# Layer 1's latents: the values' PSUM buffers, the engines that empty them, and the rotary key's copy

## The chip, the cores and the metric

The kernel runs on one core of a Trainium2 chip. A core has five engines that each work through their own queue in order: TensorE (PE: matmuls and transposes), VectorE (DVE), ScalarE (ACT), GpSimd (POOL) and SyncE (SP, which here only issues DMAs). Matmuls write to PSUM, which has eight banks of 128 partitions by 512 float32; VectorE and ScalarE carry results from there to SBUF. The metric is the device time of one execution in microseconds, as a median of several.

## The reference, cut to what matters

Two layers over a sequence of 1024 tokens with 1024 features. Layer 0 is differential attention, layer 1 is multi-head latent attention; each is followed by a gated MLP with a causal convolution. The change is in the input side of layer 1's attention:

```python
def mla_attention(h, w_in, q_norm_g, kv_norm_g, w_uq, w_ukv, w_o, cos, sin):
    proj = h @ w_in                                            # 384 + 256 + 32 columns
    c_q = rms_norm(proj[..., :MLA_Q_RANK], q_norm_g)           # the queries' latents
    c_kv = rms_norm(proj[..., MLA_Q_RANK:MLA_Q_RANK + MLA_KV_RANK], kv_norm_g)
    k_pe = apply_rope(proj[..., MLA_Q_RANK + MLA_KV_RANK:], cos, sin)   # the rotary key
    q = (c_q @ w_uq).reshape(b, s, MLA_HEADS, MLA_NOPE + MLA_ROPE)
    kv = (c_kv @ w_ukv).reshape(b, s, MLA_HEADS, MLA_NOPE + MLA_V)
    v = kv[..., MLA_NOPE:]                                     # the values
```

## The kernel before

Every product of float32 matrices is made from three matmuls (`mm3`, lines 116 to 121): both operands are split into a high part and the rest (`hi`, line 127, mostly on ACT; `lo`, line 130, on DVE or POOL), and the product of the two rests is left out. Layer 1's input (`mla_input`, line 1111) runs over eight tiles of 128 tokens. For tile i it does:

- `latents(i)`: 48 matmuls from the normed tokens into the two banks of one tile `S`: the queries' 384 columns in the first bank, the 256 key and value columns and the rotary key's 32 in the second. Then, for each of the two norms, a sum of squares on ACT (L157), its root on DVE (L162) and POOL (L163), and a scaled copy on DVE (L1151) into the SBUF tile `nat`. Last, ACT copies the 32 rotary columns (L1152).
- `turn(i)`: PE transposes `nat` (L1160, L1168, and L1169 for the rotary columns) into tiles `b`, which ACT and DVE split; ACT copies the rotary key (L1173).
- `values(i)`: 12 matmuls into a second tile `S`, one copy by ACT of all 1024 columns (L1184), and a DMA to DRAM (L1185).

Between these stand the transposes of the next tokens (L182). After the eighth tile come the key and query units of the first two heads, the rotary key's rotation (`rotary`: DVE L233, POOL L235 and L236, then ACT's L127 and DVE's L125 copies of 32 rows to the four key tiles, for each half of the tokens), and then attention, in 64 steps of scores (into `S`), softmax (L1449, L1450), POOL's scaling (L149), transposes of the weights (L248, into `b`), their split, and the product with the values (L1470 and L1471, into `u`).

The eight banks are shared by all of this through three tags:

```python
def big(self):
    return self.t(self.ps, "S", [P, 1024], 2)
def bank(self, tag="b"):
    return self.t(self.ps, tag, [P, 512], 1 if tag == "u" else 3)
```

So there are two tiles `S` of two banks, three of one bank under `b`, and one bank under `u`, which `mla_input` does not use before the change. Who follows whom in an engine's queue is not written out here: a scheduler orders the instructions of this part and of attention when the program is built, by its own estimate of when operands and buffers come free. An engine that waits at run time holds up all that is queued behind.

Of the kernel before, what the change touches and what calls it, by code (L numbers as in the profile page):

```python
# [18 lines left out]
P = 128  # L19
S = 1024  # L20
D = 1024
# [35 lines left out]
class Trunk:  # L57
# [1053 lines left out]
    def mla_input(self, W, hts, turns, v_d, heads_of):  # L1111


        nc, a = self.nc, self.a
# [24 lines left out]
        late = SimpleNamespace()  # L1139

        def latents(i):
            acc = self.big()
            for k in range(KD):
                for b, m, kind in ((0, 384, "q"), (512, 288, "kv")):
                    wh, wl = where[kind, k]
                    self.mm3(acc[:, b : b + m], hts[i][:, 0, k, :], hts[i][:, 1, k, :], wh, wl, k == 0, k == KD - 1)
            nat = nats([P, 672])
            for b, m, off, gain in ((0, 384, 0, g[0]), (512, 256, 384, g[1])):
                d = nat[:, off : off + m]
                r = self.rstd(acc[:, b : b + m], d, m)  # L1150
                nc.vector.scalar_tensor_tensor(d, acc[:, b : b + m], r, gain, ALU.mult, ALU.mult)  # L1151
            nc.scalar.copy(nat[:, 640:672], acc[:, 768:800])  # L1152
            return nat

        def turn(i, nat):
# [19 lines left out]
        def values(i):  # L1175
            half = i // 4
            s = slice((i % 4) * P, (i % 4 + 1) * P)
            y = self.big()
            for b in (0, 512):
                for k in range(2):  # L1180
                    ch, cl = (cT.kv(part, half, k)[:, s] for part in range(2))
                    self.mm3(y[:, b : b + 512], ch, cl, late.wv[k][0][:, b : b + 512], late.wv[k][1][:, b : b + 512], k == 0, k == 1)
            vs = self.raw([P, D])
            nc.scalar.copy(vs, y)  # L1184
            nc.sync.dma_start(v_d[:, :, i].rearrange("h p e -> p h e"), vs.rearrange("p (h e) -> p h e", e=P))  # L1185

        def rotary(half):
# [9 lines left out]
        nat = {}  # L1197
        for i in range(NT + 2):
            if i < NT:
                nat[i] = latents(i)  # L1200
                if turns:
                    turns.pop(0)()
            if i in (1, 5):
                latent_tiles(i // 4)
            if i == 3:
                heads = heads_of(cT, kT)
            if i == 2:
                late.tab = self.at("s13", [MLA_ROPE, 2, S])
                nc.sync.dma_start(late.tab, a["rope_k"])
            if i == 1:  # L1210

                late.wv = [self.split(f"s{4 + k}", self.fetch(a["mla_wuv"][k * P : (k + 1) * P, :], D)) for k in range(2)]
            if i == 6:
                kT += [self.at(place, [P, 2, S], F32R) for place in ("s0", "s1", "s10", "s11")]
            if 0 <= i - 1 < NT:
                turn(i - 1, nat.pop(i - 1))
            if i == NT:
                heads.first(0)
            if i >= 2:
                values(i - 2)  # L1220
            if i in (7, NT + 1):
                rotary(i // NT)
# [517 lines left out]
```

## Time and profile before

| what | us |
|---|---|
| median of 3 runs (lowest to highest) | 2480.05 (2479.67 to 2480.57) |
| span of the profiled execution | 2476.8 |
| PE busy in it | 2376.1 (96%) |
| DVE, ACT, POOL busy | 1899.8, 1301.3, 651.6 |
| mean granted PE clock | 0.992 of full speed |
| the latents' stage of layer 1 | about 1258 to 1347 |
| its tail: values, first heads' units, rotary key | 1347 to 1376 |
| attention of layer 1 | about 1376 to 1700 |

The profiled execution's own time is not listed apart from its span; the median stands 3.25 us above the span, for what lies before the first and after the last instruction. All times within the program count from the span's start. A row of the time line is: start, length, engine, line, operation, the tile written and the tiles read, and in brackets how long the engine was idle before it and what ended that. A row of the waits is: the waiting engine, tile and line, what it waited for, the total, how often, and the longest.

### The profile page before, as it was taken

The numbers are of one execution on the slowest core, as the hardware profiler recorded it, in microseconds if no ns is written. First come the engines' busy times: TensorE is split into PE (matmuls) and PEld (weight loads), VectorE is DVE, ScalarE is ACT, GpSimd is POOL, SyncE is SP. The second block draws the span as 40 slices with busy tenths as digits, with TensorE's granted clock in tenths as the row PEclk, the third lists the DMA queues.
The fourth block names the chain that finished last, engine by engine and source line by source line (L and its number), as shares of the span: only waits on it lengthen the run. The fifth ranks groups of instructions, "written<-read, shape, count | busy, mean of one in ns | idle before, by whom it ended". The sixth has DMA issues, their size and how long they took to land.

```text
span 2476.8 us, 32625 instructions
## 1 busy us (share of the span) xinstructions
PE 2376.1 (96%) x11960; PEld 2007.7 (81%) x11960; DVE 1899.8 (77%) x3078; ACT 1301.3 (53%) x2417; POOL 651.6 (26%) x512
## 2 busy tenths in 40 slices
PE   6999999899999999999999999999999999999998
PEld 5788787788888888788888788888888888887886
DVE  6667776846788888899853787777368888888997
ACT  5677777844444444444434777776244444444443
POOL 5545554526000000000131666656350000000001
PEclk9999999899999999999999999999999999999999
DMA  4111111314222222543221211113222222227401
GB/s 154 43 35 43 35 35 44 128 59 132 64 83 83 80 90 80 216 159 104 81 90 52 75 39 35 42 54 119 93 85 94 77 85 84 87 77 280 166 5 77
DMA packets 95104, 214.44 MB, mean 87 GB/s; under 512 B 8640, under 2 KB 33856, under 8 KB 94784
## 3 DMA queue, kind: packets, MB, share of 16 engines
q1 hardware_dynamic: 86048, 185.09, 22.4%
q10 hardware_dynamic: 8896, 27.27, 3.0%
q8 instruction: 94, 1.54, 0.3%
q14 instruction: 66, 0.54, 0.1%
HBM read 159.89 MB, written 52.43 MB: 86 GB/s over the span
## 4 chain that ended last, share of the span: by engine, by line
PE 77%; DVE 8%; ACT 6%; issue 3%; DMA 3%; POOL 2%; SPq 0%; ACTq 0%; POOLq 0%; DVEq 0%
PE S L119 13%; PE S L120 13%; PE S L121 13%; PE b L119 8%; PE b L120 8%; PE b L121 8%; PE u L119 3%; PE u L120 3%; PE u L121 3%; PE b L248 2%; ACT u L1381 1%; PE b L182 1%; PE u L1471 1%; PE u L1470 1%; DVE s L130 1%
## 5 line engine op out<-in xcount | busy, mean ns | idle before, releaser
L163 POOL TENSOR_TENSOR st<-st,mhalf 128x1 f32<-128x1 f32 x56 | 33.8, 605 | 1314.0 <-DVE st L162 1304.9
L127 ACT CAST u<-h 128x512 fp32r<-128x512 f32 (+2 forms) x242 | 146.1, 619 | 279.6 <-DVE h L630 255.7
L119 PE MATMUL S<-s,u 128*128 128x512 f32 (+1 forms) x752 | 285.8, 380 | 5.7 <-DVE u L768 3.9
L121 PE MATMUL S<-s,u 128*128 128x512 f32 (+1 forms) x752 | 284.1, 378 | 0.0
L120 PE MATMUL S<-s,u 128*128 128x512 f32 (+1 forms) x752 | 284.0, 378 | 0.0
L119 PE MATMUL b<-s,u 128*128 128x512 f32 x588 | 231.6, 394 | 0.5
L120 PE MATMUL b<-s,u 128*128 128x512 f32 x588 | 229.5, 390 | 0.0
L121 PE MATMUL b<-s,u 128*128 128x512 f32 x588 | 229.4, 390 | 0.0
L678 DVE SCALAR_TENSOR_TENSOR u<-u,conv,u 128x1023 f32<-128x1023 f32 (+1 forms) x176 | 225.2, 1279 | 1.6 <-ACT u L674 1.6
L149 POOL TENSOR_TENSOR u<-u,st 128x384 f32<-128x384 f32 (+7 forms) x160 | 170.1, 1070 | 152.2 <-DVE st L1456 100.8
L119 PE MATMUL u<-s,s 128*128 128x512 f32 x432 | 174.7, 404 | 14.7 <-ACT h L416 6.7
L130 DVE TENSOR_TENSOR u<-b,u 128x512 fp32r<-128x512 f32 (+1 forms) x256 | 158.7, 632 | 38.2 <-ACT u L127 35.7
L127 ACT CAST s<-u 128x512 fp32r<-128x512 f32 (+3 forms) x196 | 128.6, 693 | 96.5 <-PE u L121 35.4
L121 PE MATMUL u<-s,s 128*128 128x512 f32 x432 | 170.2, 394 | 0.0
L120 PE MATMUL u<-s,s 128*128 128x512 f32 x432 | 169.6, 393 | 0.0
L119 PEld LDWEIGHTS S<-s,u 128*128 128x128 f32 x752 | 141.4, 188 | 34.2 <-issue 4.4
L121 PEld LDWEIGHTS S<-s,u 128*128 128x128 f32 x752 | 141.4, 188 | 26.3
L120 PEld LDWEIGHTS S<-s,u 128*128 128x128 f32 x752 | 141.4, 188 | 25.9
L127 ACT CAST u<-b 128x512 fp32r<-128x512 f32 (+1 forms) x256 | 133.8, 550 | 50.1 <-PE b L248 46.3
L681 ACT ACTIVATE u<-u 128x1024 f32<-128x1024 f32 x44 | 46.7, 1062 | 197.2 <-DVE u L678 197.2
L248 PE MATMUL b<-ident,u 128*128 128x128 f32 x864 | 138.3, 277 | 7.9 <-DVE u L130 5.7
L130 DVE TENSOR_TENSOR u<-h,u 128x512 fp32r<-128x512 f32 x162 | 111.4, 688 | 33.0 <-ACT u L127 31.8
(254 smaller groups left out, 6646.5 us busy)
## 6 DMA issues: line engine op xcount, KB each, us to landing
u<-in_ffn_up SPq DMA_DIRECT2D x88, 512.0 KB, 3.8
g_d<-u ACTq DMA_DIRECT2D x44, 512.0 KB, 2.6
u<-in_ffn_down SPq DMA_DIRECT2D x66, 256.0 KB, 5.3
u<-g_d SPq DMA_DIRECT2D x62, 256.0 KB, 4.4
s<-in_da_wqkv SPq DMA_DIRECT2D x24, 512.0 KB, 3.6
x_d<-u SPq DMA_DIRECT2D x16, 512.0 KB, 2.9
s<-x_d SPq DMA_DIRECT2D x8, 1024.0 KB, 8.9
u<-o_d SPq DMA_DIRECT2D x24, 256.0 KB, 2.8
```

Of the source, the lines that this page charges most:

```text
L119: mm(out, lh, rl, start=first, stop=False, skip_group_check=onto)
L120: mm(out, lh, rh, start=False, stop=False, skip_group_check=onto)
L121: mm(out, ll, rh, start=False, stop=last, skip_group_check=onto)
L127: self.nc.scalar.copy(out, src)
L130: (eng or self.nc.vector).tensor_sub(out, src, hi.bitcast(F32))
L149: self.nc.gpsimd.tensor_mul(x, x, s.to_broadcast(list(x.shape)))
L163: nc.gpsimd.tensor_tensor(r, s, self.mhalf, ALU.pow)
L182: self.nc.tensor.transpose(ps[:, k * P : (k + 1) * P], src[:, k * P : (k + 1) * P], self.ident)
L248: self.nc.tensor.transpose(ps[:, j * P : (j + 1) * P], probs[t][:, k : k + P], self.ident)
L678: nc.vector.scalar_tensor_tensor(t[half][:, back:], u[half][:, : S - back], w, t[half][:, back:], ALU.mult, ALU.add)
L681: nc.scalar.activation(t[0], t[0], AF.Silu)
L1381: nc.scalar.activation(e, sc[c], AF.Exp, bias=nm[:, c : c + 1], accum_out=l[:, c : c + 1])
```

## The change

In `values`, the two halves of 512 columns get a single bank each, the first under `u` and the second under `b`, and each half is copied out alone, the first by VectorE and the second by ScalarE. In `latents`, the copy of the rotary key's 32 columns moves ahead of the norms and from ScalarE to VectorE.

```diff
             nat = nats([P, 672])
+            nc.vector.tensor_copy(nat[:, 640:672], acc[:, 768:800])
             for b, m, off, gain in ((0, 384, 0, g[0]), (512, 256, 384, g[1])):
                 d = nat[:, off : off + m]
                 r = self.rstd(acc[:, b : b + m], d, m)
                 nc.vector.scalar_tensor_tensor(d, acc[:, b : b + m], r, gain, ALU.mult, ALU.mult)
-            nc.scalar.copy(nat[:, 640:672], acc[:, 768:800])
             return nat
...
-            y = self.big()
-            for b in (0, 512):
+            vs = self.raw([P, D])
+            for b, tag, evict in ((0, "u", nc.vector.tensor_copy), (512, "b", nc.scalar.copy)):
+                y = self.bank(tag)
                 for k in range(2):
                     ch, cl = (cT.kv(part, half, k)[:, s] for part in range(2))
-                    self.mm3(y[:, b : b + 512], ch, cl, late.wv[k][0][:, b : b + 512], late.wv[k][1][:, b : b + 512], k == 0, k == 1)
-            vs = self.raw([P, D])
-            nc.scalar.copy(vs, y)
+                    self.mm3(y, ch, cl, late.wv[k][0][:, b : b + 512], late.wv[k][1][:, b : b + 512], k == 0, k == 1)
+                evict(vs[:, b : b + 512], y)
```

In the changed program the lines after the first insertion stand one lower up to the end of the norms, so that L1151 becomes L1152 and the rotary copy is L1148; both value copies have line 1184. The numbers behind a tile's name tell its buffers apart.

The first place is PE's queue at the fourth and fifth group of latents, before the change. S_11182 is the fourth group's tile, S_11291 the second tile of values, S_11307 the fifth group's.

```order
L121 MATMUL S_11182<-u_1872_10783,s_1904_11008 128x288
L182 MATMUL b_11246<-ident,s_1681_9117 128x128 x4
L182 MATMUL b_11253<-ident,s_1681_9117 128x128 x4
L1160 MATMUL b_11276<-ident,u_1921_11111 128x128 x3
L119 MATMUL S_11291<-s_1915_11039,s_1911_11034 128x512
...
L121 MATMUL S_11291<-s_1917_11044,s_1911_11034 128x512
L1168 MATMUL b_11284<-ident,u_1921_11111 128x128 x2
L1169 MATMUL b_11284<-ident,u_1921_11111 32x128
L119 MATMUL S_11307<-u_1864_10739,s_1926_11125 128x384
```

The same place after the change, where S_11184 is the fourth group's tile, S_11311 the fifth's, b_11175 the second half of the first values and u_11294 the first half of the second:

```order
L121 MATMUL S_11184<-u_1872_10783,s_1904_11008 128x288
L119 MATMUL S_11311<-u_1864_10739,s_1926_11125 128x384
...
L120 MATMUL S_11311<-u_1870_10779,s_1926_11125 128x384
L119 MATMUL b_11175<-s_1915_11039,s_1911_11034 128x512
...
L119 MATMUL S_11311<-u_1866_10743,s_1926_11125 128x288
L182 MATMUL b_11248<-ident,s_1681_9117 128x128 x4
L119 MATMUL u_11294<-s_1915_11039,s_1911_11034 128x512
```

The fifth group follows the fourth with nothing between, and the values' matmuls, which stood between two groups, are now strewn into a later group.

The second place is ACT's queue behind the last group of latents, before the change. S_11714, S_11803 and S_11819 are the last three tiles of values; the rows with 32x2x512 are the rotary key's copies.

```order
L1184 COPY u_2009_11727<-S_11714 128x1024
L127 COPY s_1992_11601<-u_2012_11736 32x2x512 x2
L127 COPY s_1994_11603<-u_2012_11736 32x2x512 x2
L127 CAST s_1978_11503<-b_11747 128x2x128
L1152 COPY u_2001_11685<-S_11636 128x32
L1184 COPY u_2023_11816<-S_11803 128x1024
...
L1184 COPY u_2025_11832<-S_11819 128x1024
L127 CAST u_2028_11841<-h_2026_11835 32x512
L127 CAST s_2016_11773<-h_2018_11784 128x512
L127 COPY s_1992_11601<-u_2028_11841 32x2x512 x2
L127 COPY s_1994_11603<-u_2028_11841 32x2x512 x2
```

The same after the change; b_11733, b_11824 and b_11842 are the second halves of the last three values:

```order
L1184 COPY u_2013_11724<-b_11733 128x512
L127 COPY s_1996_11609<-u_2018_11748 32x2x512 x2
L127 COPY s_1998_11611<-u_2018_11748 32x2x512 x2
L127 CAST s_1981_11509<-b_11759 128x2x128
...
L1184 COPY u_2028_11815<-b_11824 128x512
L127 COPY s_1996_11609<-u_2036_11857 32x2x512 x2
L127 COPY s_1998_11611<-u_2036_11857 32x2x512 x2
L1184 COPY u_2031_11833<-b_11842 128x512
```

The last values' copy stood ahead of the second set of rotary copies and now stands behind it.

The third place is PE's queue in attention, before the change, in a head in the middle; b_12925 to b_12949 are transposed weights of one step, u_12888 a product with the values.

```order
L248 MATMUL b_12941<-ident,u_2259_12855 128x128
L119 MATMUL S_13000<-s_1992_11601,s_2206_12624 128x384
...
L248 MATMUL b_12925<-ident,u_2265_12877 128x128
...
L248 MATMUL b_12941<-ident,u_2265_12877 128x128
L1470 MATMUL u_12888<-u_2262_12870,s_2091_12125 128x256
L1471 MATMUL u_12888<-u_2262_12870,s_2091_12125 128x256
...
L248 MATMUL b_12949<-ident,u_2259_12855 128x128
```

The same step after the change, where b_12941 to b_12965 are the four tiles of transposed weights:

```order
L248 MATMUL b_12941<-ident,u_2267_12871 128x128
...
L119 MATMUL S_13016<-s_1996_11609,s_2214_12640 128x384
...
L248 MATMUL b_12949<-ident,u_2267_12871 128x128
...
L119 MATMUL S_13057<-s_1996_11609,s_2214_12640 128x512
...
L248 MATMUL b_12957<-ident,u_2267_12871 128x128
...
L1470 MATMUL u_12904<-u_2270_12886,s_2099_12141 128x256
...
L248 MATMUL b_12965<-ident,u_2267_12871 128x128
```

Before, three tiles were filled in one run of ten transposes and the fourth, which reuses the first one's bank, came after four short matmuls; now the scores of the next steps stand between one tile and the next. No line of attention is edited: the scheduler's order differs here in every head.

## The prediction

> **What bounds the kernel now.** I read the page first, for the engine that sets the time.
>
> ```profile
> PE 2376.1 (96%) x11960; PEld 2007.7 (81%) x11960; DVE 1899.8 (77%) x3078; ACT 1301.3 (53%) x2417; POOL 651.6 (26%) x512
> PEclk9999999899999999999999999999999999999999
> PE 77%; DVE 8%; ACT 6%; issue 3%; DMA 3%; POOL 2%; SPq 0%; ACTq 0%; POOLq 0%; DVEq 0%
> ```
>
> PE is busy for 96% of the span and holds 77% of the chain that ended last, at nearly full clock. So a change pays only where it takes away a wait of PE, and what DVE or ACT save elsewhere is worth nothing. Next I asked for PE's waits over three stretches: the latents' groups (1284 to 1347), the tail and the start of attention (1347 to 1386), and attention's steady part (1440 to 1654).
>
> ```profile
> PE S L119 <- ACT u L1184: 3.3, 3, 1.4
> PE b L1168 <- DVE u L1151: 1.0, 1, 1.0
> ...
> PE S L119 <- ACT u L1450: 4.1, 4, 1.8
> PE S L119 <- ACT s L127: 1.4, 1, 1.4
> PE S L119 <- ACT u L1184: 0.8, 1, 0.8
> ...
> PE b L248 <- DVE u L130: 4.8, 9, 0.9
> ```
>
> In the latents PE loses 3.3 + 1.0 = 4.3 us, nearly all of it to the copy of the values, L1184. In the tail it loses 4.1 + 1.4 + 0.8 = 6.3 us, mostly to the softmax of attention's first steps. In attention nine waits for the split of the transposed weights make 4.8 us. The time line shows how one of the first kind comes about.
>
> ```profile
> 1299.54 1.06 ACT L157 ACTIVATE h<-s 128x1024 bf16<-128x1024 f32 x1
> 1300.59 1.00 ACT L1184 COPY u<-S 128x1024 f32<-128x1024 f32 x1
> 1301.64 0.44 PE L119 MATMUL S<-u,s 128*128 128x384 f32 x1 [1.37 <-ACT u L1184]
> ```
>
> ACT first squares a token tile (1.06 us) and only then copies the values (1.00 us). PE starts the fifth group of latents 0.05 us after that copy, having idled 1.37 us, though the fourth group's tile was long summed. The reason is the count of buffers: two tiles S serve latents and values alike, so each group waits until the values in between are out.
>
> **The change part by part.** The prices come from the groups of ACT and DVE by shape, between 1255 and 1376.
>
> ```profile
> L1184 ACT COPY u<-S 128x1024 f32<-128x1024 f32 x8 | 8.1, 1011 | 2.9 <-issue 2.1 <-PE S L121 0.8
> L127 ACT CAST s<-b 128x512 fp32r<-128x512 f32 x12 | 6.6, 587 | 0.1
> L1152 ACT COPY u<-S 128x32 f32<-128x32 f32 x8 | 1.6, 203 | 1.2 <-DVE u L1151 1.2
> L127 ACT CAST s<-u 32x1024 fp32r<-32x1024 f32 x8 | 8.4, 1047 | 0.8 <-POOL u L130 0.7
> ...
> L1268 DVE TENSOR_TENSOR h<-b,u 128x512 f32<-128x512 f32 x4 | 2.7, 683 | 2.5 <-PE b L121 2.5
> L130 DVE TENSOR_TENSOR h<-b,h 128x128 fp32r<-128x128 f32 x8 | 2.3, 288 | 1.5 <-ACT h L127 1.5
> L125 DVE CAST s<-u 32x1024 fp32r<-32x1024 f32 x8 | 5.5, 685 | 0.1
> L1448 DVE MEMSET S<- 64x64 f32 x3 | 0.3, 112 | 0.0
> ```
>
> *The copies of the values.* ACT's eight copies of 1.011 us go. For each, ACT does one half; the nearest row, a one-bank read of the same size, has 0.587. DVE does the other half, for which before has no plain copy: the nearest is its one-bank multiply with 0.683, and nothing that it runs on this size is cheaper than ACT's 0.587, so I take 0.68 with 0.5 to 0.8 as ends. ACT saves 8 x (1.01 - 0.59) = 3.4 us and DVE gets 5.4 us more. In the latents a bank of values is filled again only a whole group later, 8 us by PE's rows, so neither figure enters the sum there.
>
> *The waits for S.* The values leave S, and latents alternate between its two tiles. A group then needs the tile of the group before the last, which has been read out while 48 matmuls of the last one ran (about 7.4 us at 0.13 to 0.18 each), against some 4 us of squares, roots and scaled copies. In PE's order before, 0.3 to 1.1 us of matmuls stand between the last values and the next group; after, nothing has to be emptied there. The three waits go, **-3.3 us**. What is late next: PE's transposes of the normed tokens, but these stand 2 us or more ahead of their use in the new order. The 1.0 us for L1168 behind L1151 goes too, **-1.0 us**, since that transpose now stands a whole group behind the norm.
>
> *The rotary columns.* ACT's eight copies of 0.203 us go; DVE makes them at once, at a price between its 0.112 (a fill of 64x64) and 0.288 (128x128); I take 0.2. They add a wait: in the new program the first square of each group (L157) waits for this copy, for both write the tile `nat`. Behind that square in ACT's queue stand the splits of the transposes. So each group's norm ends about 0.2 us later, hidden by the 7 us of matmuls in all groups but the last, where it counts below.
>
> *The tail.* I walk the new order from the end of the last group with durations of before, where that end is 1347.3. A matmul of 512 columns counts 0.23 from start to start, as in the two rows of 1348, a transpose 0.105 (ten of them take 1.01 to 1.06 to the next row in the view on attention below).
>
> ```profile
> 1347.57 0.49 ACT L157 ACTIVATE u<-S 128x384 f32<-128x384 f32 x1 [7.17 <-PE b L1169]
> 1348.10 0.40 PE L119 MATMUL S<-s,s 128*128 128x512 f32 x1
> 1348.33 0.39 PE L120 MATMUL S<-s,s 128*128 128x512 f32 x1
> 1348.42 0.55 POOL L163 TENSOR_TENSOR st<-st,mhalf 128x1 f32<-128x1 f32 x1 [9.47 <-DVE st L162]
> 1350.39 1.38 POOL L163 TENSOR_TENSOR st<-st,mhalf 128x1 f32<-128x1 f32 x1
> 1353.16 0.48 DVE L1151 SCALAR_TENSOR_TENSOR u<-S,st,h 128x256 f32<-128x256 f32 x1
> ...
> 1361.21 1.01 ACT L1184 COPY u<-S 128x1024 f32<-128x1024 f32 x1 [2.13 <-issue]
> 1365.51 0.34 SPq L135 DMA_DIRECT2D u<-v_d  x1
> 1376.37 0.79 PE L119 MATMUL S<-s,s 128*128 128x512 f32 x1 [0.25 <-ACT u L1450]
> ```
>
> Before, the chain is: square at +0.3, root, scaled copy, and the same for the second norm; DVE's four rotary copies (4 x 0.685) get in between and stretch POOL's root from 0.55 to 1.38, so the second scaled copy runs at +5.9. After, it runs at about +6.7, because the rotary copy (0.2) and the half of the values (0.68) stand ahead of it on DVE. PE reaches its transpose (L1168) already at 6 x 0.105 + 12 x 0.23 + 3 x 0.105 + 6 x 0.23 = +5.1, since only half of the next values stands between; that is **a new wait of about 2 us**, counted in what follows. ACT's half copy of values ends at +4.1 and its four rotary copies (4 x 1.047) at +8.3; behind the splits of the last transposes, the last values' first half starts at about +9.5 against +10.5, and the rotary rotation that hangs on L1173 starts near +10.4 against +12.2. ACT does not sit behind two more full copies, so the first score of 896 columns, which before starts at 1376.37 = +29.1, comes at about +28, and 0.7 us of transposes that stood behind it are done by then, while 0.5 us of transposes that stood ahead of the last group have moved into the tail. That is 1.1 + 0.7 + 0.5: **-2.3 us**. One thing runs the other way: the last values' copy by ACT now stands behind the second rotary copies and ends near +22 (before, 1362.2 = +14.9). Behind it are the store, the fetch of the values back (SP, 1365.51) and ACT's split of them, which now comes at about +28.5 and has exps queued behind it. That is why I bound the tail at 2 us lost and 4.5 us won.
>
> *Attention.* No line is edited, but the scheduler orders it anew. A step's four tiles of transposed weights share three banks:
>
> ```profile
> 1477.89 1.25 PE L248 MATMUL b<-ident,u 128*128 128x128 f32 x10
> 1478.58 1.07 ACT L127 CAST u<-b 128x512 fp32r<-128x512 f32 x2 [1.22 <-PE b L248]
> 1478.90 0.36 PE L1470 MATMUL u<-u,s 128*128 128x256 f32 x1
> 1479.20 0.56 DVE L1449 TENSOR_REDUCE st<-S 128x1 f32<-128x384 f32 x1
> 1479.68 1.28 DVE L130 TENSOR_TENSOR u<-b,u 128x512 fp32r<-128x512 f32 x2
> 1480.41 0.55 PE L248 MATMUL b<-ident,u 128*128 128x128 f32 x3 [0.86 <-DVE u L130]
> ```
>
> Ten transposes run in one go, four products follow, and the fourth tile waits 0.86 us for the first one's bank: ACT's split, then a maximum (0.56) and two subtractions on DVE. Summing PE's rows from the end of the first tile to the fourth (a matmul by its columns, 0.06 to 0.23) gives 1.0 us before, against a turnround of 1.2 to 1.9 (1.0 plus waits of 0.18 and 0.86 in turn). In the new order the scores between the tiles make it 2.4 us, and the smallest such distance on any bank is 2.0 us; a distance of 1.7 us elsewhere in the old order shows no wait. But DVE's new order puts a maximum ahead of the first subtraction, so the turnround grows to about 2.1. Of the 4.8 us I take 3.4 as gone: **-3.4 us**, with 0 and 5 as ends.
>
> **Sum.** -3.3 - 1.0 - 2.3 - 3.4 = -10.0 us, from a span of 2476.8 to 2466.8. The median of the runs lies 3.25 us above that span, so **2470.0 us**, 0.40% less. About 0.2% (5 us) is what a measurement of this kernel can tell from no change.
>
> **The clock.** The granted clock is a cost that the order of the waits decides.
>
> ```profile
> core 0: us, PE busy (x) PEld busy (x) DVE busy (x) ACT busy (x) POOL busy (x), PEclk, DMA share, GB/s
> 1357.06:1360.48 3.42, 2.64 (x10) 1.91 (x11) 2.86 (x7) 1.68 (x5) 0.22 (x1) 1.00 0.56 158
> 1370.72:1374.13 3.41, 1.62 (x9) 1.03 (x7) 3.36 (x5) 3.39 (x6) 2.45 (x2) 1.00 0.00 0
> 1374.13:1377.55 3.42, 2.31 (x8) 1.71 (x7) 3.34 (x9) 2.11 (x7) 3.42 (x2) 0.50 0.41 153
> 1377.55:1380.96 3.41, 3.41 (x12) 2.83 (x11) 1.79 (x4) 1.95 (x4) 3.41 (x4) 0.50 0.52 154
> ```
>
> A stretch of 3.41 us in which PE was busy 1.62 is followed by two at half clock, while one with 2.64 is not. Half clock over the 5.7 us of busy time behind it costs 2 to 3 us. The sum leaves it as it is, for the new walk has two waits of over 1 us between +25 and +28, as before. The Trainium skill, "TensorE: Matmul & The Clock Gate", Part 1, says that the array falls back to half rate after an idle window of about 3.4 us that runs freely, and advises against gaps above that. The length of the stretches agrees; the gap does not, since here 1.79 us of waiting was enough. By the page no wait of the new tail would cost any clock, and the sum would be 2467.5; by the rows it stays 2470.0.
>
> **The rivals.**
>
> *A second fall of the clock, and no gain in attention.* The new wait of 2 us for L1168 falls within one such stretch and halves the clock: 3 us of the time back. With attention's waits staying too, -6.6 + 3 = -3.6 us, 2476.4. For it: 1.79 us of waiting did it at 1374. Against: the 2 us must lie in one stretch, and the distances in attention's order are plain.
>
> *No fall at all.* The tail's new waits (2, 0.5, 1.2 and 1.3 us) are spread over five or more stretches, and none holds 1.8 us of them: 2.5 us of the old loss go as well, 2467.5. For it: the 1.36 us of waiting in the stretch at 1357 cost nothing. Against: the last two waits are within 3.4 us of each other. The page above speaks for it, the row at 1370 against.
>
> *The tail takes it all.* The values come back 7 us later, exps queue behind their split, and the gain of the latents only lengthens waits that end at a fixed time: 4.3 + 2.3 us are lost, attention keeps its 3.4 or not: 2476.7 to 2480. For it: ACT's queue is strict. Against: the chain through POOL's rotation, which set the start before, gets shorter.
>
> *Slower.* The new order of attention puts a wait into every head. The place is the fourth tile of weights, where DVE's maximum stands ahead of the subtraction that frees the bank. If two maxima and a late split come together, the turnround is 1.9 + 0.56 + 0.64 = 3.1 us against a distance of 2.0: 1.1 us in each of 14 heads, 15.4 us in place of the 4.8. The sum is then -6.6 - 4.8 + 15.4 = +4.0, 2484.1, and with a second such place in a head over 2490. It decides from (6.6 + 4.8) / 14 = 0.8 us a head. Against: the longest turnround seen is 1.9.
>
> *The change does nothing.* The scheduler could have kept values and latents in turn. Its order shows otherwise, and it would give 2480.
>
> **How the numbers follow.** The forecast has 0.48 (2465 to 2474), no fall 0.12, the second fall 0.18, the tail 0.13, slower 0.06, nothing 0.03. The range for 8 in 10 takes in the ends of tail and attention on the side of the forecast and most of the second fall: 2464 to 2478. Faster by over 0.2% (below 2475.1): the forecast, no fall, and half of the second fall, 0.70 in all with a little of the tail. Same: 0.25. Slower: 0.05.
>
> **What would show it.** In the changed trace, no wait for L1184 ahead of a group of latents, and the last group's end near 1342.5 (0.5 us of transposes moved behind it). One wait for L1168 of some 2 us behind it. Attention's first score of 896 columns near 1370.5. In attention, waits for L130 under 1.5 us in all. The prediction is wrong if PE waits for DVE's copy under `u`, if the clock falls twice, or if a wait comes back in every head.

## The result, and the profile after

| | before | after |
|---|---|---|
| median, us (lowest to highest) | 2480.31 (2479.67 to 2484.03) | 2462.72 (2462.70 to 2463.07) |
| ratio, 95% interval | | 0.9929 (0.9915 to 0.9943) |
| span of the profiled execution, us | 2476.8 | 2460.9 |

The change takes 17.6 us off, 0.71%. The forecast was 2470.0 us, 10 us less than before; the time lies 1.3 us below the range. The span fell by 15.9 us only: every listed run stands 1.8 us above its own span, so the profiled execution of before took about 2478.6 us, 1.7 us less than its median. So only 1.8 of the 3.25 us between before's median and its span lie outside the first and the last instruction; the rest is the distance of that one execution from the median. The page of after, in the same three lines as before:

```profile
PE 2372.5 (96%) x11960; PEld 2008.6 (82%) x11960; DVE 1898.7 (77%) x3094; ACT 1298.3 (53%) x2409; POOL 650.5 (26%) x512
PEclk9999999899999999999999999999999999999999
PE 80%; DVE 7%; ACT 5%; DMA 3%; issue 3%; POOL 2%; SPq 0%; POOLq 0%; ACTq 0%; DVEq 0%
```

PE still sets the time. Where the 15.9 us of span went is read from four stretches, cut at the same work in both kernels: the *latents* (from the first 288-column matmul of layer 1 to 0.2 us behind the start of the last one), the *tail* (to the 81st product of attention with the values, L1470 and L1471), the *heads* (to the 441st, nine heads) and the *last heads* (to the 640th, the last). The view gives, for each stretch, its length and every engine's busy time with its count of rows. Before:

```profile
core 0: us, PE busy (x) PEld busy (x) DVE busy (x) ACT busy (x) POOL busy (x), PEclk, DMA share, GB/s
1259.11:1347.36 88.25, 83.89 (x533) 79.54 (x532) 34.46 (x76) 33.56 (x91) 20.40 (x24) 1.00 0.20 62
1347.36:1433.29 85.93, 79.02 (x431) 66.62 (x430) 64.47 (x143) 64.42 (x127) 50.57 (x38) 0.96 0.22 68
1433.29:1628.73 195.44, 190.37 (x1224) 169.28 (x1222) 154.52 (x377) 141.66 (x312) 123.42 (x100) 1.00 0.13 37
1628.73:1735.11 106.38, 99.46 (x632) 87.86 (x631) 79.15 (x181) 72.72 (x156) 64.99 (x49) 0.98 0.32 100
```

After:

```profile
1261.02:1343.07 82.05, 82.05 (x527) 79.14 (x527) 37.35 (x86) 31.09 (x82) 20.39 (x24) 1.00 0.20 64
1343.07:1431.18 88.11, 79.67 (x437) 67.95 (x435) 65.60 (x151) 63.14 (x129) 51.01 (x39) 0.96 0.22 66
1431.18:1617.32 186.14, 185.54 (x1220) 167.84 (x1218) 152.39 (x374) 141.69 (x310) 123.82 (x99) 1.00 0.14 39
1617.32:1718.09 100.77, 98.34 (x635) 86.83 (x634) 78.42 (x183) 73.17 (x157) 62.62 (x49) 1.00 0.33 105
```

The latents lose 6.2 us and have no wait left (PE busy 82.05 of 82.05). The tail gains 2.2. The heads, where no line is edited and the granted clock is 1.00 in both kernels, lose 9.3 us, and the last heads 5.6. That is 18.9 us; 1.9 us more before the first of these stretches and 1.1 behind the last leave 15.9. One thing stands out: PE's idle time (length less busy) falls by 11.8 us, from 23.3 to 11.5, and its *busy* time by 7.1, from 452.7 to 445.6, though the matmuls in the four stretches are the same but for 0.5 us. So much of what was lost before does not show as idle.

PE's waits after, by the view that was read for the forecast, the longest of each stretch. In the latents there is none. In the tail (1342 to 1380, then 1380 to 1440), the heads and the last heads:

```profile
PE S L119 <- ACT u L1450: 3.4, 2, 2.2
PE b L1168 <- DVE u L1152: 1.6, 1, 1.6
PE u L119 <- ACT s L127: 0.4, 1, 0.4
...
PE S L119 <- ACT u L1450: 1.5, 1, 1.5
PE b L119 <- DVE u L130: 1.0, 2, 0.7
...
PE b L248 <- DVE S L1448: 0.3, 1, 0.3
...
PE b L248 <- DVE u L130: 0.7, 1, 0.7
PE b L119 <- DVE u L130: 0.4, 1, 0.4
...
```

The new wait in the tail, 1.6 us for L1168, is the one foreseen. Of the waits for L130 in the heads (eight, with 4.2 us; the forecast's ninth lies behind them) none is left; the heads' only wait is one of 0.3 us for a fill by DVE (L1448). The new copies, from the groups by shape (line, engine, operation, tiles, shapes, count, then busy time and mean ns of one):

```profile
L1184 DVE COPY u<-u 128x512 f32<-128x512 f32 x8 | 5.5, 682 | 0.5 <-PE u L121 0.3 <-DMA v_d<-u 0.2
L1148 DVE COPY u<-S 128x32 f32<-128x32 f32 x8 | 1.5, 191 | 20.5 <-PE S L121 20.2 <-PE b L1169 0.3
...
L1184 ACT COPY u<-b 128x512 f32<-128x512 f32 x8 | 4.7, 586 | 3.1 <-PE b L121 2.1 <-ACT u L157 1.0
```

They cost what was taken for them: 0.682 us (0.68), 0.191 (0.2) and 0.586 (0.59).

### The profile page after: what moved, and what is told of

Same layout as the page of the kernel before. It is cut to its first block, busy times and chain, and to the rows that moved or that the text cites. A ratio compares the mean times of both kernels' runs of the same rounds, so it can differ in the third digit from the quotient of the medians.

```text
span 2460.9 us, 32675 instructions
## 1 busy us (share of the span) xinstructions
PE 2372.5 (96%) x11960; PEld 2008.6 (82%) x11960; DVE 1898.7 (77%) x3094; ACT 1298.3 (53%) x2409; POOL 650.5 (26%) x512
## 4 chain that ended last, share of the span: by engine, by line
PE 80%; DVE 7%; ACT 5%; DMA 3%; issue 3%; POOL 2%; SPq 0%; POOLq 0%; ACTq 0%; DVEq 0%
PE S L119 13%; PE S L121 13%; PE S L120 13%; PE b L119 8%; PE b L120 8%; PE b L121 8%; PE u L119 3%; PE u L120 3%; PE u L121 3%; PE b L248 3%; PE u L1471 1%; PE b L182 1%; PE u L1470 1%; ACT u L1381 1%; ACT u L127 1%
## 5 line engine op out<-in xcount | busy, mean ns | idle before, releaser
L119 PE MATMUL u<-s,s 128*128 128x512 f32 x448 | 182.7, 408 | 14.1 <-ACT h L416 6.7
L130 DVE TENSOR_TENSOR u<-b,u 128x512 fp32r<-128x512 f32 (+1 forms) x256 | 158.0, 630 | 35.3 <-ACT u L127 33.4
L121 PE MATMUL u<-s,s 128*128 128x512 f32 x448 | 177.7, 397 | 0.0
L120 PE MATMUL u<-s,s 128*128 128x512 f32 x448 | 177.0, 395 | 0.0
L130 DVE TENSOR_TENSOR u<-h,u 128x512 fp32r<-128x512 f32 x162 | 111.4, 687 | 32.6 <-ACT u L127 31.5
```

What stands on the lines that cost most here:

```text
L119: mm(out, lh, rl, start=first, stop=False, skip_group_check=onto)
L120: mm(out, lh, rh, start=False, stop=False, skip_group_check=onto)
L121: mm(out, ll, rh, start=False, stop=last, skip_group_check=onto)
L130: (eng or self.nc.vector).tensor_sub(out, src, hi.bitcast(F32))
```

## The experiments

The open question was whether the edits, which touch the latents and the tail, or the new order that the scheduler gave attention made the time. Variants of the change show that attention's order on PE comes in a few kinds only: between the 121st and the 441st product, before's has 80 groups of transposes, the changed kernel's 72, and a small edit of the latents decides which one a kernel gets. So both can be had with and without either edit.

**Theory A**: the edits make the gain. **Theory B**: most of it is attention's order. A diff is against the changed kernel unless said otherwise.

*Values alone, order of before.* The rotary copy goes back to ACT, behind the norms:

```diff
-            nc.vector.tensor_copy(nat[:, 640:672], acc[:, 768:800])
...
+            nc.scalar.copy(nat[:, 640:672], acc[:, 768:800])
             return nat
```

> Only the values' part of the change: two single banks, half copied by DVE and half by ACT; the rotary key's columns are copied by ACT at the end, as before. The scheduler gives it before's order of attention (PE's rows from the 121st to the 600th product are the same ones as before's). Theory A (what is edited gives the gain: the latents, their tail and the half copies; attention's order is worth the 3.4 us of its one wait): 2480.3 - 17.6 + 3.4 + 1 for the missing rotary copy, so 2467 to 2469. Theory B (most of the gain is the order of attention and of the last heads, 8 + 6 us, which came along without being edited): latents 5 to 6 us earlier and nothing after them, so 2473.5 to 2476.

*Rotary columns alone, order of after.* The values go back to `S` and one copy by ACT:

```diff
-            for b, tag, evict in ((0, "u", nc.vector.tensor_copy), (512, "b", nc.scalar.copy)):
-                y = self.bank(tag)
...
+            y = self.big()
+            for b in (0, 512):
...
+            nc.scalar.copy(vs, y)
```

> Only the rotary key's columns copied by DVE at once; the values stay in S (two banks, one copy by ACT). The scheduler gives it the changed kernel's order of attention. Theory A: the wait for S ahead of the latents stays, 1 us of the rotary copy and 3.4 us of attention go, so 2475 to 2477. Theory B: the latents keep before's waits and attention with its last heads is 12 to 14 us shorter, so 2466 to 2469.

*Both edits, engines exchanged, order of before.*

```diff
-            for b, tag, evict in ((0, "u", nc.vector.tensor_copy), (512, "b", nc.scalar.copy)):
+            for b, tag, evict in ((0, "u", nc.scalar.copy), (512, "b", nc.vector.tensor_copy)):
```

> Both parts of the change, with the two engines exchanged: the half under u copied by ACT, the half under b by DVE. The work is the same to the instruction count, but the scheduler gives it before's order of attention. Theory A: 2463 to 2466, like the changed kernel. Theory B: like the kernel with the values' part alone, 2472.5 to 2476, since nothing of attention's gain is there.

*Values in S, copy cut in half, order of after.* Against before:

```diff
-            nc.scalar.copy(vs, y)
+            nc.vector.tensor_copy(vs[:, :512], y[:, :512])
+            nc.scalar.copy(vs[:, 512:], y[:, 512:])
```

> Values in S as before and the rotary columns copied by ACT as before; only the copy of the values out of S is cut in half between DVE and ACT. PE's order is before's up to the end of the latents and the changed kernel's in attention. Theory A: S comes free some 0.3 us earlier for 4 of the groups, 1 us, and attention 3.4 us: 2475 to 2477. Theory B: 2465 to 2469, attention and its last heads being 12 to 14 us shorter.

*Before, with the transposed rotary key (L1173) copied by DVE: a third order.* Against before:

```diff
-            nc.scalar.copy(kp[half][:, s], ps[:MLA_ROPE, 256:384])
+            nc.vector.tensor_copy(kp[half][:, s], ps[:MLA_ROPE, 256:384])
```

> The kernel before with this one copy by DVE and no part of the change. The latents keep before's order in PE's queue up to the last group, and the scheduler makes a third order of attention from it: 71 groups of transposes and 195 switches between transposes and products from the 121st to the 441st product, against 80 and 208 before and 72 and 196 after, and the next transposes of a bank mostly 1.9 us or more behind the last ones. If the order of attention is the gain: the stage from the 81st to the 441st product 186 us, the next one to the 640th 101 us, and 2465 to 2470 in all. If the edits are: within 1 us of before, 2479 to 2481.

The table has the medians, the ratios to the runs of before that were made beside each (medians 2480.19 to 2480.72 here and below), and the four stretches of each profiled execution in us, by the view shown above.

| kernel | attention's order | median (lowest to highest) | ratio, 95% interval | latents | tail | heads | last heads |
|---|---|---|---|---|---|---|---|
| before | before's | 2480.31 (2479.67 to 2484.03) | | 88.3 | 85.9 | 195.4 | 106.4 |
| values alone | before's | 2474.74 (2471.17 to 2476.90) | 0.9974 (0.9963 to 0.9984) | 82.0 | 85.6 | 195.4 | 106.7 |
| engines exchanged | before's | 2475.43 (2472.39 to 2477.46) | 0.9978 (0.9969 to 0.9987) | 82.0 | 84.9 | 195.4 | 106.5 |
| rotary alone | after's | 2465.63 (2463.25 to 2466.34) | 0.9937 (0.9925 to 0.9950) | 86.9 | 87.0 | 186.0 | 101.0 |
| copy cut in half | after's | 2471.95 (2469.96 to 2475.49) | 0.9968 (0.9956 to 0.9981) | 88.4 | 91.4 | 185.6 | 100.9 |
| before, L1173 by DVE | a third | 2469.83 (2469.32 to 2471.24) | 0.9956 (0.9944 to 0.9969) | 88.0 | 89.8 | 187.3 | 100.7 |
| after | after's | 2462.72 (2462.70 to 2463.07) | 0.9929 (0.9915 to 0.9943) | 82.1 | 88.1 | 186.1 | 100.8 |

Theory B holds. The latents' 6.2 us come with the single banks and with nothing else (82.0 in three kernels, 86.9 to 88.4 without). The heads take 195.4 us in all three kernels with before's order and 185.6 to 187.3 in all four without it, whatever is edited. The rotary copy alone, an edit priced at a fifth of a microsecond per tile, is worth 14.9 us by the medians (2480.51 to 2465.63); by its stretches, -9.5 in the heads, -5.4 in the last heads, -1.3 in the latents and +1.1 in the tail. The values' part alone, in before's order, is worth 5.8 us (2480.51 to 2474.74). The two do not add up, 20.7 us against 17.6: they share 1.3 us of the latents, and with both edits the tail is longer than the two alone would make it. With both edits in the program, the exchange of two engines costs 12.8 us (2475.43 against 2462.61, the changed kernel's median when run again).

Two expectations of theory B missed. The rotary columns alone were to take 2466 to 2469 and took 2465.63, a little less. The cut copy was to take 2465 to 2469 and took 2471.95, which is in neither theory's range. Its heads are as expected; its tail is 91.4 us, 5.5 longer than before's, with two stretches at half clock in it, of 6.8 us each, where before has one of them.

*What a change from transposes to products costs.* From the 121st to the 441st product, PE changes 160 times between transposes and other matmuls in before's order and 144 times in after's. (The 208 and 196 of an expectation above count the changes between scores, units and products too.) Could that be the busy time that went? PE alone, all else left out:

```diff
+        for kind, most in (("V", 64), ("S", 32)):
+            for k in (1, 2, 4, 16, 32):
+                for _ in range(32 // k):
+                    do("T", 4 * k)
+                    do(kind, most * k // 32)
```

> PE alone, nothing of the reference is computed (the output is a constant of the test): 128 transposes of 128x128 and 64 products of 256 columns in 32, 16, 8, 2 and 1 groups, then 128 transposes and 32 products of 512 columns likewise, with nothing to wait for. Theory W (the old order loses at its stops alone): the stretches of one kind are equally long within 2%, 0.4 us. Theory C (each change from transposes to products costs 0.1 us or more with no wait, as the rows of attention suggest, 0.15 in the old order and 0.09 in the new): 32 groups take 3 to 5 us longer than one.

In the time line, 32 groups of four transposes (L1507) and two products of 256 columns (L1509) run from 21.61 to 43.23, and 16 groups of eight and four from 48.70 to 70.33, each followed by a filler (L1511):

```profile
21.61 0.60 PE L1507 MATMUL b<-ident,e 128*128 128x128 f32 x4
21.97 0.48 PE L1509 MATMUL u<-x,v 128*128 128x256 f32 x2
...
43.23 5.63 PE L1511 MATMUL S<-x,v 128*128 128x512 f32 x24
48.70 1.03 PE L1507 MATMUL b<-ident,e 128*128 128x128 f32 x8
...
70.33 2.00 PE L1511 MATMUL S<-x,v 128*128 128x512 f32 x8
```

21.62 against 21.63 us, and the other three groupings take 21.59 to 21.65. With products of 512 columns, 32 groups take 21.44 us and one group 21.24, which is under 0.01 us a group. So a change costs next to nothing, and theory W stands, as to the price of a change. The test also gives the rates: 0.675 us for four transposes and two products, so 0.105 and 0.12 to 0.13 us each.

*What a stop costs.* PE writes a bank (four transposes), DVE copies it, PE does n products elsewhere and needs the bank again:

```diff
+        for count in (20, 12, 11, 10, 9, 8, 7, 6, 5, 4, 2):
+            for rep in range(8):
+                for j in range(4):
+                    keep(nc.tensor.transpose(bank[:, j * P : (j + 1) * P], e[:, j * P : (j + 1) * P], ident))
+                nc.vector.tensor_copy(scratch[rep % 4], bank)
+                products(count)
```

> PE and DVE alone, nothing of the reference is computed: four transposes into one bank, DVE copies the bank, PE does 2 to 20 products of 256 columns and wants the bank again. Theory I (the idle time in the waits is what a stop costs): the period less PE's work (4 x 0.105 + n x 0.12) is the idle time shown, within 0.03 us. Theory M (the rows' modelled lengths hide the start of every wait): the loss is 0.15 to 0.25 us more than the idle time shown in each period with a wait, and a wait below 0.15 us shows none.

| products n | 12 | 9 | 8 | 7 | 6 | 5 | 4 | 2 |
|---|---|---|---|---|---|---|---|---|
| PE's work, 0.42 + 0.12 n | 1.86 | 1.50 | 1.38 | 1.26 | 1.14 | 1.02 | 0.90 | 0.66 |
| period | 1.87 | 1.51 | 1.44 | 1.44 | 1.44 | 1.44 | 1.44 | 1.44 |
| lost | 0.01 | 0.01 | 0.06 | 0.18 | 0.30 | 0.42 | 0.54 | 0.78 |
| idle shown for PE | 0 | 0 | 0 | 0 | 0 | 0.19 | 0.31 | 0.55 |
| idle shown for PEld | 0 | 0 | 0 | 0.16 | 0.28 | 0.40 | 0.52 | 0.75 |

The period does not fall below 1.44 us here, the bank's turnround through DVE. The rows of idle time are from the time line, which leaves out gaps under 0.15 us. Theory M stands: PE's idle time hides 0.23 us of each wait in this test, as it expected. At n = 6 as well: six periods, 8.64 us, have PE busy for 8.21, so 0.07 us of each wait of 0.30 are left, too little for the view. So waits of up to 0.30 us are not listed, where theory M expected 0.15. The weight loads, PEld, show the loss to 0.03 us where it is 0.18 us or more. Two periods, n = 7 and n = 5:

```profile
148.25 0.66 PE L1518 MATMUL b<-ident,e 128*128 128x128 f32 x4
148.66 1.07 PE L1508 MATMUL u<-x,v 128*128 128x256 f32 x7
148.94 0.69 DVE L1519 COPY c<-b 128x512 f32<-128x512 f32 x1 [0.75 <-PE b L1518]
149.68 0.14 PEld L1518 LDWEIGHTS b<-ident,e 128*128 128x128 f32 x1 [0.16 <-DVE c L1519]
149.68 0.33 PE L1518 MATMUL b<-ident,e 128*128 128x128 f32 x1
...
180.33 0.42 PEld L1518 LDWEIGHTS b<-ident,e 128*128 128x128 f32 x4 [0.40 <-DVE c L1519]
180.33 0.66 PE L1518 MATMUL b<-ident,e 128*128 128x128 f32 x4 [0.19 <-DVE c L1519]
```

Seven products need 7 x 0.12 = 0.84 us but stand in the time line with 1.07, up to 149.73: their row runs past the start of the next transposes at 149.68, though PE had waited for DVE in between.

*Versions that may beat both.* In the changed kernel, ACT copies both halves (`act2r`, run twice), DVE copies L1173 (`kpdve`), and both (`best`). All three have the changed kernel's order of attention.

```diff
-            nc.scalar.copy(kp[half][:, s], ps[:MLA_ROPE, 256:384])
+            nc.vector.tensor_copy(kp[half][:, s], ps[:MLA_ROPE, 256:384])
...
-            for b, tag, evict in ((0, "u", nc.vector.tensor_copy), (512, "b", nc.scalar.copy)):
+            for b, tag, evict in ((0, "u", nc.scalar.copy), (512, "b", nc.scalar.copy)):
```

> The whole change, but ACT copies both halves of the values. The order of attention is the changed kernel's, and the latents differ from its order in PE's queue only behind the seventh group. If the gain is the single banks and attention's order, the engine that copies does not matter: 2462 to 2465. If the half on DVE matters (ACT's second copy of about 0.65 us stands in front of the squares and splits of every tile), 8 copies and the tail give 3 to 6 us back: 2466 to 2469.

> The changed kernel with one thing more: the copy of the transposed rotary key, 32 rows of 128 (L1173), by DVE in place of ACT. Attention's order stays. The tail of the changed kernel is 2.2 us longer than that of the values' part alone; if that hangs on ACT's queue, 1 to 2 us of it go: 2460.5 to 2462. If the tail hangs on the chain through POOL's rotation and the copies of the second half, nothing moves: 2462 to 2464.

> The changed kernel once more, on the chip on which the next two run: 2462 to 2465.

> The whole change with both halves of the values copied by ACT, beside the changed kernel on one chip. Its tail was 84.8 us against 88.1, its latents and attention the same within 0.3. If DVE's half copy costs the tail something (the scaled copies of the norms queue behind it), it is 2 to 3 us below the changed kernel, 2460 to 2462; if the tail's difference was chance, within 1 us.

> Both halves of the values by ACT and the copy of the transposed rotary key (L1173) by DVE, in the changed kernel: DVE and ACT change places, 8 copies of 32 rows for 8 of 512 columns. If the two alone (2460.6 and 2459.7, on the other chip run) add up: 2457 to 2459. If either only got a better tail by the order that the scheduler made of it, no better than the better of them: 2459 to 2463.

| kernel | median (lowest to highest) | ratio to before, 95% interval | latents | tail | heads | last heads |
|---|---|---|---|---|---|---|
| both halves by ACT | 2460.59 (2458.95 to 2462.89) | 0.9918 (0.9905 to 0.9932) | 82.0 | 84.8 | 186.2 | 101.0 |
| L1173 by DVE | 2459.67 (2458.58 to 2460.98) | 0.9912 (0.9899 to 0.9926) | 82.0 | 89.1 | 185.9 | 100.9 |
| after, again | 2462.61 (2460.08 to 2463.62) | 0.9928 (0.9916 to 0.9941) | 82.1 | 86.9 | 186.1 | 100.7 |
| both halves by ACT, again | 2458.47 (2458.02 to 2459.35) | 0.9915 (0.9901 to 0.9929) | 82.0 | 86.1 | 186.2 | 101.1 |
| both edits | 2459.73 (2457.13 to 2460.35) | 0.9916 (0.9903 to 0.9930) | 82.1 | 85.0 | 185.8 | 100.8 |

The last three ran on one chip. Both halves by ACT is 4.1 us below the changed kernel there, with ranges that do not touch, so the half on DVE gains nothing here, and the 3 to 6 us that it might have been worth were a wrong guess. Both runs of this variant came out below either alternative of their expectations (2462 or more, then 2460 or more). That it is better by itself is less sure: on the other chip its runs reach up to 2462.89, and the intervals of the ratios overlap. The two edits do not add up. Why ACT alone would be better stays open: the stretches of the two profiled executions differ by 0.8 us in the tail, and the rest lies outside them. That the tail hangs on ACT's queue is not borne out: with L1173 on DVE it is 89.1 us. Neither alternative of that expectation holds, since the total came out below both. (Its comparison was off too: the changed kernel's tail is 2.5 us longer than that of the values' part alone, 88.1 against 85.6; 2.2 is the difference to before.)

## Why the prediction was wrong, step by step

*The waits for S and L1168.* Forecast -3.3 - 1.0 (and 0.5 us of transposes moved out); the stretch lost 6.2 us. The mechanism was right and no wait is left. PEld's waits in it were 4.3 and 1.5 us, 5.8 in all, where PE's gave 4.3: the stops were priced 1.5 us too low, and with the 0.5 that makes 6.3.

*The tail.* Forecast -2.3 with 2 lost as the bound; it came out at +2.2, or +1.0 in the second execution (86.9). The walk met its marks: the last group begins its last matmul at 1342.87 (forecast end near 1342.5), the wait for L1168 is 1.6 us (2), and the first score of 896 columns starts at 1370.74 (1370.5). That the times of day agree is partly luck: the latents began 1.9 us later than before's and took 1.4 us less than forecast. From the end of the last group the score comes at +27.7 (28), 1.3 us sooner than before's +29.0. What the walk left out is behind that mark: from there to the 81st product before takes 56.9 us and the changed kernel 60.4, 3.5 us more. The next score waits another 2.16 us for the exp, and more waits follow by 1440. Part of the 3.5 us is the half clock, of which 2.2 us lay ahead of the mark before and nothing now. Against the foreseen condition, the clock did fall twice, but each time for one stretch of 3.41 us in place of one fall of two, so the time at half clock is the same 6.8 us. The view by stretches, after:

```profile
1372.22:1375.63 3.41, 1.25 (x6) 1.05 (x6) 1.22 (x3) 2.45 (x4) 1.68 (x1) 1.00 0.04 16
1375.63:1379.04 3.41, 3.41 (x14) 3.09 (x13) 1.56 (x5) 2.32 (x5) 3.41 (x4) 0.51 0.49 149
...
1385.87:1389.28 3.41, 1.53 (x12) 1.32 (x13) 3.12 (x8) 3.34 (x9) 3.41 (x3) 1.00 0.60 183
1389.28:1392.69 3.41, 3.41 (x18) 3.31 (x17) 2.49 (x8) 1.87 (x6) 3.30 (x4) 0.51 0.40 101
```

Again a stretch with PE busy for less than half of it (1.25 and 1.53 of 3.41) is followed by one at half clock. It is no sure rule: in before, the stretch from 1251.25 to 1254.66 has PE busy for 1.64 us, about as little as the 1.62 at 1370.72, and the next one is at full clock. The forecast also misread a row here: of the 1.36 us of waiting that it puts into the stretch at 1357, which cost no clock, 0.63 us lie ahead of it, and PE idled 0.78 us in it (3.42 less 2.64). The rival without any fall did not come about. The Trainium skill, "TensorE: Matmul & The Clock Gate", speaks for that rival in Part 1, but in the section "A second HAM failure mode: psum-queue depth-cycling" it tells of a kernel whose frequent short idles between groups made the clock swing between full and half rate; these rows agree with that.

*Attention.* **This is the step that failed**: "Of the 4.8 us I take 3.4 as gone". Attention lost 14.9 us. That the stops would go was right; their price was not. The forecast took PE's idle time, 4.8 us up to 1654. The same stretch of before read by PEld, in the heads (1433 to 1629):

```profile
PEld b L248 <- DVE u L130: 5.3, 8, 1.0
PEld b L119 <- DVE s L130: 1.4, 4, 0.4
PEld S L119 <- ACT u L1450: 1.4, 4, 0.3
PEld u L1470 <- DVE h L1474: 0.7, 4, 0.2
PEld b L119 <- DVE u L130: 0.4, 1, 0.4
```

and after (1431 to 1617):

```profile
PEld b L119 <- PE b L248: 0.5, 1, 0.5
PEld b L248 <- PE u L1471: 0.4, 1, 0.4
```

9.2 us against 0.9: that is 8.3 of the 9.3 us, and the new order has 1.0 us of matmuls less in this stretch, by counting them at their rates (0.55 of it stands in the last heads). From the 121st product to the 441st the two kernels have the same 1088 matmuls, shape by shape, in another order. There before takes 174.93 us and the changed kernel 166.41, and PEld's waits are 8.8 and 0.4 us: 8.4 of the 8.5 us. Thirteen of the 21 waits are on lines for which PE's own view lists none. One of them, before:

```profile
1472.25 0.69 DVE L130 TENSOR_TENSOR s<-b,s 64x512 fp32r<-64x512 f32 x1
1472.37 0.52 PE L248 MATMUL b<-ident,u 128*128 128x128 f32 x3
...
1473.00 0.19 PEld L119 LDWEIGHTS b<-s,u 128*128 128x128 f32 x1 [0.35 <-DVE s L130]
1473.00 0.50 PE L119 MATMUL b<-s,u 128*128 128x512 f32 x1
```

Three transposes take 3 x 0.105 = 0.32 us, so PE was done at 1472.69 and waited until DVE had emptied a bank at 1472.94; the row's 0.52 us cover most of it. The Trainium skill, "Perfetto Trace Analysis", "Tensor Engine Instruction (MATMUL, LD_WEIGHTS)", says that the end of a matmul in a trace is estimated from its size and not observed. The stop experiment agrees, and gives the size of the error there: 0.23 us a stop.

The second half of the same step is that it ended at 1654, and the heads after that stood in no term. There PEld's waits fall from 10.1 to 5.2 us (the sum of the lists for 1628.7 to 1735.1 and 1617.3 to 1718.1), and the length by 5.6. Part of the rest is the clock: before has one stretch of 3.41 us at half clock there (0.98 in the mean), which by this costs at most 1.7 us, and after has none.

*The sum read the other way.* PEld's waits over all four stretches fall by 5.8 in the latents, 8.3 in the heads and 4.9 in the last heads, and rise by 1.0 in the tail (10.1 to 11.1): 18.0 us of the 18.9 that the stretches lost. PE's idle time gives 11.8.

*The rivals.* A wait in every head did not come, and the tail did not take it all: it gave back 2.2 of the 21.1 us of the other stretches. The clock fell a second time, but not with attention's waits kept, and the time at half clock did not grow. That the change might gain most where it edits nothing was in no rival; attention's order was weighed only for the waits that PE's view showed.

What stays open is why the scheduler chooses one order or the other. It was seen only that moving one small copy to another engine is enough (the rotary columns, or L1173), or dividing the values' copies otherwise. No kernel had attention's order changed with the rest of the program the same to the row, and the orders of DVE and ACT, which the scheduler also sets, were not varied apart from PE's.

## What to carry to other kernels

Where PE sets the time, read what stops cost from the waits of the weight loads or from starts of rows, not from PE's idle time. Where a scheduler orders the program, compare the order of parts that were not edited, and test an edit beside a twin that does the same work in the other order: here the exchange of two engines undid 12.8 of 17.6 us.

## What the runs showed of the hardware

PE's changes between transposes and products, for which one theory expected 0.1 us each, cost under 0.01 us in the test. And the place of the half-clock stretches moves from one execution to the next: the part of the program before the latents, in which PE's order is the same in all these kernels, took between 1258.6 us (values alone) and 1264.8 (both halves by ACT). The kernel with both halves by ACT took 1264.8 us in one profiled execution and 1259.2 in the other, on another chip. The 19 us just before the latents in these two:

```profile
1245.70:1264.70 19.00, 14.69 (x59) 11.66 (x58) 11.45 (x17) 5.92 (x9) 7.26 (x4) 0.82 0.36 136
...
1240.10:1259.10 19.00, 14.69 (x73) 11.96 (x72) 13.06 (x17) 5.92 (x9) 7.61 (x5) 1.00 0.31 114
```

A granted clock of 0.82 against 1.00. So the 1.9 us by which the changed kernel reaches its latents later than before's need not be an effect of the change. Runs of one kernel spread by up to 6.5 us (17 runs of before, 2478.77 to 2485.25).

The traces also show how little idle time a fall takes. Cut into stretches of 3.41 us along the falls, from 30 to 2440 us, the twelve profiled executions of whole kernels have 53 falls from full to half clock. Every stretch at full clock with PE busy for less than 1.49 us was followed by one, none with more than 1.85 us was, and between the two it went both ways.
